# A hybrid decoder-layer step on one core: output projection in products of 512 columns, and three pieces of work moved behind the last token tile

## The chip, the core and the metric

The kernel runs on one NeuronCore of a Trainium2 chip. A core has five engines that run their own instruction queues in order: PE (TensorE, matrix products; its weight loads are listed as PEld), DVE (VectorE), ACT (ScalarE), POOL (GpSimd) and SP (SyncE, here only for starting transfers). ACT and POOL start transfers too. The metric is device microseconds (us) of one execution, as the median of the runs.

## The reference, cut to what matters

One inference step of one decoder layer, for a prompt of 512 tokens and a batch of 8 sequences with 8 new tokens each, so 576 token rows of width 1024. Two attention branches (`o_fox`, `o_nsa`) are computed first, from the inputs, the weights and a paged cache. What follows them is where the change lies:

```python
def post_mixer(x, pm, o_fox, o_nsa, lp):
    br_fox = jnp.einsum('btk,kd->btd', o_fox.reshape(b, t_len, FOX_QW), lp['w_br_fox'])
    br_nsa = jnp.einsum('btk,kd->btd', o_nsa.reshape(b, t_len, NSA_QW), lp['w_br_nsa'])
    mix = pm['g_fox'] * br_fox + pm['g_nsa'] * br_nsa
    x = x + pm['gt1'] * jnp.einsum('btd,de->bte', mix, lp['w_out'])
    h = rms_norm(x, lp['norm2_g']) * (1.0 + pm['sc2']) + pm['sh2']
    u = jax.nn.relu(jnp.einsum('btd,df->btf', h, lp['w_up']))
    return x + pm['gt2'] * jnp.einsum('btf,fd->btd', u * u, lp['w_down'])
```

`w_out` is 1024 x 1024, `w_up` 1024 x 4096, `w_down` 4096 x 1024. All data are float32. The outputs are the two `y` and the new cache rows.

## The kernel before, in words

**Precision.** A float32 operand is cut into a high and a low part of the type that PE multiplies (`split`, line 131 for the low part on DVE, line 112 for the high part on ACT). A product is then three products: high by high, low by high and high by low. For the 64 sample tokens a tile of 128 rows holds high and low rows together, so that two products do.

**Stages.** Input projection, compressed keys, prompt attention, sample attention, gates and branches (`mix_part`), then the four that matter here: the output projection (`out_part`), the first quarter-way of up (`up_first`), the rest of up (`mlp_up`) and down (`mlp_down`).

**Output projection.** Five token tiles, in the order 0, 4, 1, 2, 3 (tile 4 holds the sample tokens; tile 3 is the last). The stationary operand is `mix2` (tokens), the moving one `w_out`. The weight comes in four parts `wo0` to `wo3`, each 256 columns by all eight 128-row blocks, with a high and a low half (`wo1h`, `wo1l`). A token tile makes four groups of products of 256 columns, each into a PSUM bank of its own, and after each group DVE multiplies the bank by the gate (`wot`) and adds it to the residual `x`. When a tile's four groups are done, its rows are stored (`x2D`, POOL's queue) and normalised: ACT sums the squares (`nsq`; for the last tile `n`), DVE runs a chain of 13 small instructions (`ntx` to `nrs`) for the inverse root and scales the rows. PE turns the result (`nt`) some groups later, ACT applies scale and shift (`nv`), and the pair is split into `h3H`, `h3L` or `h`, the operands of up. ACT also stores `nv` to DRAM (`hvD`).

**First features of up.** `up_first` computes features 0 to 767 as six parts of 128 (`wu1`, `wu2`, `wu3` hold two parts each), for two halves of 288 tokens. Parts 0 to 3 run first for the first half of the tokens, which needs tiles 0, 1 and a part of 4; between the second and the third of these PE turns the last tile (`nt<-identF,n`), and ACT writes its parts into a buffer `R`. Then parts 0 to 3 run for the second half (`h`, which needs tiles 2 and 3), then parts 4 and 5 (`wu3`, the late feature weights) for both halves. Each group of 24 products fills one of four PSUM banks, and ACT empties it into `u`. The raw weights (`wur`) come over SP's queue into three buffers, so the fourth load waits until the first part has been split.

**Token differences and sums.** The rest of up runs features in pairs of 128 by a scheme of seven products in place of eight. It needs differences of token quarters (`R<-R` and their splits `T0` to `T3`; `moving_sums`, line 2077) and sums of weight quarters (`sums<-pu`; `pair_weights`, line 2102). For the differences the parts of tiles 0, 1, 2 and 4 are read back from `hvD` into `R` by two transfers on POOL's queue; those of tile 3 are written by ACT.

**What sets the order.** The kernel is written in one order, and a scheduler that runs when the kernel is built places the instructions of each engine by a modelled timeline. Three things bind it: on PE a chain (`link`) that keeps products in the written order in these stages; `issue_after`, which puts an instruction behind a named one; and buffers, whose next writer waits for the last reader. `self.normed` names the two splits that a tile's `norm_parts` made last.

Of the kernel before, what the change touches and what calls it, by code (L numbers as in the profile page):

```python
# [6 lines left out]
F32 = mybir.dt.float32  # L7
# [4 lines left out]
OP = mybir.AluOpType  # L12
AX = mybir.AxisListType

P = 128
# [4 lines left out]
NS = 64  # L20
# [25 lines left out]
class Step:  # L46
# [86 lines left out]
    def rsqrt(self, out, ss, inv):  # L133

        sh = list(out.shape)
        tag = "_".join(map(str, sh[1:]))
        x, h, t = [self.small.tile(sh, F32, tag=f"nt{a}{tag}", name=f"nt{a}{self.turn}") for a in "xht"]
        i = self.small.tile(sh, I32, tag=f"nti{tag}", name=f"nti{self.turn}")
        self.turn += 2
        self.ts(x, ss, inv, EPS, OP.mult, OP.add)  # L140
        self.ts(h, x, -0.5, None, OP.mult)
        self.ts(i, x.bitcast(I32), 1, None, OP.logical_shift_right)
        self.ts(i, i, -1.0, float(0x5F3759DF), OP.mult, OP.add)
        y = i.bitcast(F32)
        for n in range(3):
            self.tt(t, y, y, OP.mult)
            self.tt(t, t, h, OP.mult)
            self.stt(out, t, 1.5, y, OP.add, OP.mult)
            y = out

# [644 lines left out]
    def rows_mm(self, pb, i, n, terms, c0=0):  # L795

        if i < 4:
            h, l = slice(P * i, P * i + P), slice(NT + NS + P * i, NT + NS + P * i + P)
            todo = [(a[:, s], w) for a, (wh, wl) in terms for s, w in ((h, wh), (l, wh), (h, wl))]
        else:  # L800
            todo = [(a[:, SEQ:SEQ + P], w) for a, ws in terms for w in ws]
        for c, (a, w) in enumerate(todo):
            self.mm(pb[:, 0:n], a, w, c == 0, c == len(todo) - 1)
# [1163 lines left out]
    def out_weights(self, q, raw=None, pin=None):  # L1967

        return self.stream(raw, self.cols(self.I["w_out"], 256 * q, 256), [P, NK, 256], "wo", q, raws=2 if raw else 0,
                           room=self.place_of(q, f"wo{q}", NK), pin=pin)  # L1970

    def out_part(self, pw, mix2, x2, h3):
# [8 lines left out]
        for i in (0, 4, 1, 2, 3):  # L1981
            m = TILES[i][1]
            for q in range(4):
                if (i, q) in turn_at:
                    rest.pop(turn_at[i, q])()
                c0 = 256 * q
                pb = self.mmb(f"wo{q}_{i}")
                self.rows_mm(pb, i, 256, [(mix2[:, k], (ws[q][0][:, k, :], ws[q][1][:, k, :])) for k in range(NK)])
                if g is None:
                    g = gp = self.gate_prompt(pw, 16, 0.5, "1")  # L1990
                t = pw.tile([P, 256], F32, tag="wot", bufs=2, name=f"wot{q}_{i}")
                if i < 4:
                    self.tt(t, pb[:, 0:256], g[:, c0:c0 + 256], OP.mult)
                else:
                    self.fold(t[:m], pb[:, 0:256], pw.tile([NS, 256], F32, tag="fold", bufs=1, name=f"fold{q}"))
                    self.tt(t[:m], t[:m], g[:m, c0:c0 + 256], OP.mult)
                self.tt(x2[:m, i, c0:c0 + 256], x2[:m, i, c0:c0 + 256], t[:m], OP.add)
# [12 lines left out]
    def up_first(self, pu, h3):  # L2010
# [4 lines left out]
        def weights(q):  # L2015
            return self.stream(None, self.cols(self.I["w_up"], P * q, P), [P, NK, P], "wu", f"{q}", raws=0,
                               parts=1, room=[w[:, NK * (q % 2):NK * (q % 2) + NK] for w in t[q // 2]])
# [11 lines left out]
        for grp in range(2):  # L2029
            for q in range(4):  # L2030
                up(q, grp, ws[q])
                if grp == 0 and q == 1:
                    R = self.pb.tile([P, NK, NT], F32, tag="x", bufs=1, name="R")
                    for h in range(2):
                        self.dma("gpsimd", R[:, 4 * h:4 * h + 4, 0:self.COL[3]], self.hvD[:, 4 * h:4 * h + 4])
                    self.norm_parts(3, h3, self.n3, lambda h: R[:, 4 * h:4 * h + 4, self.COL[3]:NT], False)
            if grp == 0:
                self.chain = None
        self.moving_sums(pu, R)
        ws = [weights(q) for q in range(4, 6)]  # L2040
# [36 lines left out]
    def moving_sums(self, pu, R):  # L2077
# [3 lines left out]
        for n, (out, a, b) in enumerate(((b11, b12, b11), (b12, b22, b12), (b22, b22, b11), (b21, b21, b22))):  # L2081
            self.tt(out, a, b, OP.subtract)
# [31 lines left out]
    def mlp_up(self, pu, h3):  # L2114
# [10 lines left out]
        def ready(n):  # L2125
            with ExitStack() as c:
                for i in (self.splits[-1], self.last_high) if n == FIRST + 1 else ():
                    c.enter_context(self.tc.issue_after(i))
# [311 lines left out]
```

## Time and profile before

| | |
|---|---|
| median of 3 runs | 1203.73 us (1199.81 to 1206.84) |
| the profiled execution | 1203.84 us |
| its span, first to last instruction | 1202.0 us |
| PE busy | 1156.1 us, 96% of the span |
| DVE, ACT, POOL busy | 770.0, 559.0, 154.7 us |
| mean granted PE clock | 0.991 |

Times in the trace run from the first instruction. A row of a timeline has the start, the time from start to end in us, the engine, the line, the operation, what it writes and reads, and how many instructions are merged; in brackets stands the idle time before it and what ended it. A row of a table by stretches of time has the stretch, its length, the busy time of each engine with the instructions that started in it, the PE clock that was granted (1.00 is full), the mean busy share of the 16 DMA engines and their rate. The chain of waits follows the work that ended last back to its start, and has a start, a length and what filled it.

### The profile page before, as it was taken

What the parts mean: (1) busy time and instruction counts of PE and PEld (TensorE: products, weight loads), DVE (VectorE), ACT (ScalarE), POOL (GpSimd) and SP (SyncE); (2) the same over time, 40 slices, a digit from 0 to 9 for tenths busy, and PEclk for the clock granted to TensorE, in tenths of its full rate; (3) what the DMA queues carried; (4) which work ended last, traced back from release to release, by engine and by line L of the source; (5) the groups of instructions that cost most, each with busy time, mean ns of one, the idle gap of its engine ahead of it and who ended that gap; (6) DMA issues with size and microseconds to landing.
All of it is one profiled execution on the core that took longest, in us unless ns stands there. A gap on an engine that the chain in (4) does not pass through costs nothing.

```text
span 1202.0 us, 24863 instructions
## 1 busy us (share of the span) xinstructions
PE 1156.1 (96%) x9335; PEld 1003.1 (83%) x9335; DVE 770.0 (64%) x1990; ACT 559.0 (47%) x1187; POOL 154.7 (13%) x172
## 2 busy tenths in 40 slices
PE   3899999999999999999999999998999999999998
PEld 3887789999666656777899999998999997888886
DVE  3678785685888856666543445667667844655586
ACT  2455463444777864545523233364556655222230
POOL 1012100000321130000300000001464500000000
PEclk9999999999999999999999999999999999999999
DMA  9599456896785348999863333354444545445302
GB/s 212 159 258 248 158 151 200 259 306 218 224 269 167 114 166 264 316 307 319 211 162 80 80 97 126 103 163 167 144 147 147 172 147 188 146 169 185 110 28 79
DMA packets 168826, 215.37 MB, mean 179 GB/s; under 512 B 18297, under 2 KB 140610, under 8 KB 166530
## 3 DMA queue, kind: packets, MB, share of 16 engines
q1 hardware_dynamic: 147650, 174.21, 46.6%
q0 software_dynamic: 9216, 25.16, 6.7%
q10 hardware_dynamic: 11840, 14.42, 4.0%
q8 instruction: 73, 1.20, 0.4%
q14 instruction: 47, 0.39, 0.1%
HBM read 190.11 MB, written 44.53 MB: 195 GB/s over the span
## 4 chain that ended last, share of the span: by engine, by line
PE 83%; DMA 5%; DVE 5%; SPq 3%; ACT 3%; issue 2%; ACTq 0%; DVEq 0%; POOLq 0%
PE dn L77 16%; PE z L77 9%; PE mg L77 8%; PE hid L77 6%; PE br L77 4%; PE wo L77 4%; PE ss L77 2%; SPq L155 2%; PE up L77 2%; PE ct L83 2%; PE k L83 2%; DMA cpg<-in_cache_nsa_kv 2%; PE ada L77 2%; PE so L77 2%; PE sp L83 1%
## 5 line engine op out<-in xcount | busy, mean ns | idle before, releaser
L77 PE MATMUL z<-winh,h 128*128 128x264 f32 (+1 forms) x576 | 110.9, 286 | 0.3
L77 PEld LDWEIGHTS z<-winh,h 128*128 128x128 f32 x576 | 91.7, 190 | 2.1 <-DVE h L787 0.9
L77 PE MATMUL z<-winl,h 128*128 128x264 f32 (+1 forms) x320 | 88.1, 284 | 0.0
L112 ACT ACTIVATE xh<-ct 128x256 fp32r<-128x256 f32 x128 | 48.0, 385 | 61.1 <-PE ct L83 36.4
L77 PE MATMUL mg<-hH,wml 128*128 128x288 f32 x256 | 75.3, 296 | 0.9 <-DVE wml L131 0.9
L77 PE MATMUL mg<-hH,wmh 128*128 128x288 f32 x256 | 75.3, 296 | 0.0
L100 DVE TENSOR_TENSOR acc<-acc,dn 128x512 f32<-128x512 f32 x60 | 41.2, 687 | 49.4 <-PE dn L77 49.3
L77 PE MATMUL mg<-hL,wmh 128*128 128x288 f32 x256 | 72.6, 294 | 0.0
L131 DVE TENSOR_TENSOR xl<-ct,xh 128x256 fp32r<-128x256 f32 x128 | 51.6, 420 | 16.6 <-ACT xh L112 14.8
L77 PEld LDWEIGHTS z<-winl,h 128*128 128x128 f32 x320 | 60.6, 190 | 0.0
L83 PE MATMUL ct<-identF,ro 128*128 128x128 f32 x256 | 37.1, 286 | 22.4 <-DVE ro L115 22.2
L131 DVE TENSOR_TENSOR wml<-wmr,wmh 128x1024 fp32r<-128x1024 f32 x14 | 17.1, 1225 | 55.9 <-ACT wmh L112 55.9
L83 PEld LDWEIGHTS ct<-identF,ro 128*128 128x128 f32 x256 | 30.7, 149 | 25.3 <-DVE ro L115 18.7
L77 PEld LDWEIGHTS mg<-hH,wml 128*128 128x128 f32 x256 | 48.1, 188 | 1.1 <-DVE wml L131 1.1
L77 PEld LDWEIGHTS mg<-hH,wmh 128*128 128x128 f32 x256 | 48.1, 188 | 0.2
L77 PEld LDWEIGHTS mg<-hL,wmh 128*128 128x128 f32 x256 | 47.2, 188 | 0.1
L131 DVE TENSOR_TENSOR wp<-sums,wp 128x1024 fp32r<-128x1024 f32 x26 | 38.2, 1474 | 11.7 <-ACT wp L112 10.9
L77 PE MATMUL hid<-xh,w1hlk 128*128 128x512 f32 (+1 forms) x160 | 45.4, 372 | 0.1
L77 PE MATMUL hid<-xh,w1hlv 128*128 128x512 f32 (+1 forms) x160 | 45.0, 367 | 0.5 <-ACT xh L112 0.4
L112 ACT ACTIVATE mgt<-mg 128x288 f32<-128x288 f32 x32 | 12.9, 410 | 58.5 <-PE mg L77 58.5
L112 ACT ACTIVATE u<-u 128x1152 f32<-128x1152 f32 x29 | 33.7, 1161 | 10.0 <-DVE u L100 9.3
L131 DVE TENSOR_TENSOR wp<-pu,wp 128x512 fp32r<-128x512 f32 (+1 forms) x26 | 27.2, 1050 | 16.9 <-ACT wp L112 16.9
(1163 smaller groups left out, 3644.3 us busy)
## 6 DMA issues: line engine op xcount, KB each, us to landing
adw<-in_w_ada SPq DMA_DIRECT2D x16, 1024.0 KB
foxD<-in_cache_fox_kv SPq DMA_DIRECT2D x128, 128.0 KB
wdr<-in_w_down SPq DMA_DIRECT2D x32, 512.0 KB
cpg<-in_cache_nsa_kv SPq DMA_DIRECT2D x120, 128.0 KB
fr<-foxD SPq DMA_DIRECT2D x28, 512.0 KB
sr<-in_cache_nsa_kv SPq DMA_DIRECT2D x112, 128.0 KB
pu<-in_w_up SPq DMA_DIRECT2D x26, 512.0 KB
uD<-u ACTq DMA_DIRECT2D x16, 576.0 KB
```

Source lines behind the costliest of these rows:

```text
L77: ins = self.nc.tensor.matmul(out, a, b, start=start, stop=stop, skip_group_check=True)
L83: ins = self.nc.tensor.transpose(out, in_, self.identF[:n, :n])
L100: self.nc.vector.tensor_tensor(out, a, b, op=op)
L112: return self.nc.scalar.activation(out, in_, f, **kw)
L131: self.splits.append((eng or self.nc.vector).tensor_tensor(l, x, h.bitcast(F32), op=OP.subtract).ins)
L155: self.issued[eng] = getattr(self.nc, eng).dma_start(out, in_).ins
```

## The change

It has four parts.

1. `out_weights`, `rows_mm`, `out_part`: the four parts of `w_out` are now 512 columns by four row blocks. Part q holds row half q % 2 and column half q // 2. A token tile makes two groups of products of 512 columns; each runs through two weight parts into one PSUM bank and is taken up once, by DVE instructions of 512 columns.
2. `up_first`: the weights of feature parts 4 and 5 (`wu3`) are written ahead of the token differences, and their splits are pinned behind `self.normed`, the last splits of the last token tile.
3. `moving_sums` and `ready`: the four token differences, and the first sums and weight splits of the pair scheme, are pinned behind the same instructions.
4. The two transfers from `hvD` to `R` (columns 0 to 447) become four: columns 0 to 319 (tiles 0, 1, 4) for both halves, then 320 to 447 (tile 2) for both.

```diff
+    def pinned(self, pins):
+        with ExitStack() as c:
+            for i in pins or ():
+                c.enter_context(self.tc.issue_after(i))
+            yield
...
     def out_weights(self, q, raw=None, pin=None):
-        return self.stream(raw, self.cols(self.I["w_out"], 256 * q, 256), [P, NK, 256], "wo", q, raws=2 if raw else 0,
-                           room=self.place_of(q, f"wo{q}", NK), pin=pin)
+        w = self.I["w_out"][:, 512 * (q % 2):512 * (q % 2) + 512]
+        return self.stream(raw, self.cols(w, 512 * (q // 2), 512), [P, 4, 512], "wo", q, raws=2 if raw else 0,
+                           room=self.place_of(q, f"wo{q}", 4), pin=pin)
...
-                pb = self.mmb(f"wo{q}_{i}")
-                self.rows_mm(pb, i, 256, [(mix2[:, k], (ws[q][0][:, k, :], ws[q][1][:, k, :])) for k in range(NK)])
+                if q % 2 == 0:
+                    pb = self.mmb(f"wo{q}_{i}")
+                self.rows_mm(pb, i, 512, [(mix2[:, 4 * (q % 2) + k], (ws[q][0][:, k, :], ws[q][1][:, k, :])) for k in range(4)],
+                             part=(q % 2, 2))
...
+                if q % 2 == 0:
+                    continue
+                t = pw.tile([P, 512], F32, tag="wot", bufs=2, name=f"wot{q}_{i}")
                 if i < 4:
-                    self.tt(t, pb[:, 0:256], g[:, c0:c0 + 256], OP.mult)
+                    self.tt(t, pb, g[:, cs], OP.mult)
...
-                    for h in range(2):
-                        self.dma("gpsimd", R[:, 4 * h:4 * h + 4, 0:self.COL[3]], self.hvD[:, 4 * h:4 * h + 4])
+                    for a, e in ((0, self.COL[2]), (self.COL[2], self.COL[3])):
+                        for h in range(2):
+                            self.dma("gpsimd", R[:, 4 * h:4 * h + 4, a:e], self.hvD[:, 4 * h:4 * h + 4, a:e])
...
+        ws = [weights(q, self.normed) for q in range(4, 6)]
         self.moving_sums(pu, R)
-        ws = [weights(q) for q in range(4, 6)]
...
-            self.tt(out, a, b, OP.subtract)
+            with self.pinned(self.normed):
+                self.tt(out, a, b, OP.subtract)
...
-            with ExitStack() as c:
-                for i in (self.splits[-1], self.last_high) if n == FIRST + 1 else ():
-                    c.enter_context(self.tc.issue_after(i))
+            with self.pinned((self.splits[-1], self.last_high) if n == FIRST + 1 else self.normed if n == FIRST else ()):
```

How the instructions stand on three engines, of the kernel before and of the changed one.

PE in the first token tile of the output projection, before: the end of the first group (`wo0`), the turns for the gate (`gp`), the start of the second group.

```order
L77 MATMUL wo_0_10835<-wo0h,mix_9234 128x256 x2
L77 MATMUL wo_0_10835<-wo0l,mix_9234 128x256
L83 MATMUL gp_10861<-identF,modT 128x128 x4
L83 MATMUL gp_10867<-identF,modT 128x128 x4
L77 MATMUL wo_0_10876<-wo1h,mix_9234 128x256 x2
L77 MATMUL wo_0_10876<-wo1l,mix_9234 128x256
```

The same place in the changed kernel:

```order
L77 MATMUL wo_0_10835<-wo0h,mix_9234 128x512 x2
L77 MATMUL wo_0_10835<-wo0l,mix_9234 128x512
L83 MATMUL gp_10849<-identF,modT 128x128 x4
L83 MATMUL gp_10855<-identF,modT 128x128 x4
L77 MATMUL wo_0_10835<-wo1h,mix_9234 128x512 x2
L77 MATMUL wo_0_10835<-wo1l,mix_9234 128x512
```

The products are twice as wide and half as many, and those with `wo1` go on in the bank that those with `wo0` began (10835 in both).

ACT at the end of the output projection and the start of up, before: splits of the weights (`wu2h`, `wu3h`), the last tile's squares (`n`), tile 2's parts (`nv`, `h<-nv`, their stores), and the last tile's parts (`R<-nt`).

```order
L112 ACTIVATE wu2h<-wur_0_11665 128x1024
L112 ACTIVATE wu3h<-wur_0_11922 128x1024
L112 ACTIVATE n_10797,nss_3_11574<-x_10779 128x1024
L112 ACTIVATE nv_0_11600<-nt_20_11595,modT,coef_10833 128x128 x4
L112 ACTIVATE nv_1_11613<-nt_21_11608,modT,coef_10833 128x128 x4
L112 ACTIVATE wu3h<-wur_0_11926 128x1024
L112 ACTIVATE h_10790<-nv_0_11600 128x4x128
L155 DMA hvD<-nv_0_11600 128x4x128
L112 ACTIVATE h_10790<-nv_1_11613 128x4x128
L155 DMA hvD<-nv_1_11613 128x4x128
L112 ACTIVATE R<-nt_30_11724,modT,coef_10833 128x128 x4
L112 ACTIVATE R<-nt_31_11735,modT,coef_10833 128x128 x4
```

The same place in the changed kernel:

```order
L112 ACTIVATE wu2h<-wur_0_11395 128x1024
L112 ACTIVATE n_10797,nss_3_11304<-x_10779 128x1024
L112 ACTIVATE nv_0_11330<-nt_20_11325,modT,coef_10833 128x128 x4
L112 ACTIVATE nv_1_11343<-nt_21_11338,modT,coef_10833 128x128 x4
L112 ACTIVATE h_10790<-nv_0_11330 128x4x128
L162 DMA hvD<-nv_0_11330 128x4x128
L112 ACTIVATE h_10790<-nv_1_11343 128x4x128
L162 DMA hvD<-nv_1_11343 128x4x128
L112 ACTIVATE R<-nt_30_11456,modT,coef_10833 128x128 x4
L112 ACTIVATE R<-nt_31_11467,modT,coef_10833 128x128 x4
L112 ACTIVATE h_10790<-R 128x4x128 x2
L112 ACTIVATE wu3h<-wur_0_11634 128x1024
```

Both `wu3h` have moved from ahead of the last tile's parts to behind them; the second follows directly, and then five `u<-up`, which empty PSUM banks. Before, two of the `u<-up` stood between the two `h<-R`.

DVE from the last tile's scaling (`n`) on, before: the first weight sum, a `wu3` split, tile 2's splits (`h<-nv`), the first token difference (`R<-R`), the last tile's splits (`h<-R`), the next sum, and the split of the first difference (`T0l`).

```order
L104 TENSOR_SCALAR n_10797<-x_10779,nrs_3_11576 128x1024
L2102 TENSOR_TENSOR sums<-pu_0_12042 128x512
L131 TENSOR_TENSOR wu3l<-wur_0_11926,wu3h 128x1024
L131 TENSOR_TENSOR h_10790<-nv_0_11600,h_10790 128x4x128
L131 TENSOR_TENSOR h_10790<-nv_1_11613,h_10790 128x4x128
L100 TENSOR_TENSOR R<-R 128x4x288
L131 TENSOR_TENSOR h_10790<-R,h_10790 128x4x128 x2
L2102 TENSOR_TENSOR sums<-pu_0_12042,pu_1_12043 128x512
L131 TENSOR_TENSOR T0l<-R,T0h 128x1152
```

The same place in the changed kernel:

```order
L104 TENSOR_SCALAR n_10797<-x_10779,nrs_3_11306 128x1024
L131 TENSOR_TENSOR h_10790<-nv_0_11330,h_10790 128x4x128
L131 TENSOR_TENSOR h_10790<-nv_1_11343,h_10790 128x4x128
L131 TENSOR_TENSOR h_10790<-R,h_10790 128x4x128 x2
L2116 TENSOR_TENSOR sums<-pu_0_11774 128x512
L131 TENSOR_TENSOR wu3l<-wur_0_11634,wu3h 128x1024
L2116 TENSOR_TENSOR sums<-pu_0_11774,pu_1_11775 128x512
L131 TENSOR_TENSOR wu3l<-wur_0_11638,wu3h 128x1024
L100 TENSOR_TENSOR R<-R 128x4x288
```

All four splits of `h` now stand directly behind `n`, and the first token difference stands behind both `wu3` splits. The other `wu3l` stood ahead of the chain that leads to `n` before.

More of the change, by code (lines that the diff above doesn't have):

```diff
@@ L1 @@
-from contextlib import ExitStack, nullcontext
+from contextlib import ExitStack, contextmanager, nullcontext
 import concourse.bass as bass
@@ L149, in rsqrt @@
             y = out
+    @contextmanager
+    def pinned(self, pins):
[3 more added lines that the diff above has]
+            yield
     def dma(self, eng, out, in_):
@@ L793, in fold, with rows_mm @@
         self.tt(out, x[0:NS], t, OP.add)
-    def rows_mm(self, pb, i, n, terms, c0=0):
+    def rows_mm(self, pb, i, n, terms, part=(0, 1)):
         if i < 4:
@@ L802, in rows_mm @@
         for c, (a, w) in enumerate(todo):
-            self.mm(pb[:, 0:n], a, w, c == 0, c == len(todo) - 1)
+            self.mm(pb[:, 0:n], a, w, c == part[0] == 0, c == len(todo) - 1 and part[0] == part[1] - 1)
     def zc(self, c0, n):
@@ L1985, in out_part @@
                     rest.pop(turn_at[i, q])()
-                c0 = 256 * q
-                pb = self.mmb(f"wo{q}_{i}")
-                self.rows_mm(pb, i, 256, [(mix2[:, k], (ws[q][0][:, k, :], ws[q][1][:, k, :])) for k in range(NK)])
+                cs = slice(512 * (q // 2), 512 * (q // 2) + 512)
+                if q % 2 == 0:
+                    pb = self.mmb(f"wo{q}_{i}")
+                self.rows_mm(pb, i, 512, [(mix2[:, 4 * (q % 2) + k], (ws[q][0][:, k, :], ws[q][1][:, k, :])) for k in range(4)],
+                             part=(q % 2, 2))
                 if g is None:
                     g = gp = self.gate_prompt(pw, 16, 0.5, "1")
-                t = pw.tile([P, 256], F32, tag="wot", bufs=2, name=f"wot{q}_{i}")
+                if q % 2 == 0:
+                    continue
+                t = pw.tile([P, 512], F32, tag="wot", bufs=2, name=f"wot{q}_{i}")
                 if i < 4:
-                    self.tt(t, pb[:, 0:256], g[:, c0:c0 + 256], OP.mult)
+                    self.tt(t, pb, g[:, cs], OP.mult)
                 else:
-                    self.fold(t[:m], pb[:, 0:256], pw.tile([NS, 256], F32, tag="fold", bufs=1, name=f"fold{q}"))
-                    self.tt(t[:m], t[:m], g[:m, c0:c0 + 256], OP.mult)
-                self.tt(x2[:m, i, c0:c0 + 256], x2[:m, i, c0:c0 + 256], t[:m], OP.add)
+                    self.fold(t[:m], pb, pw.tile([P, 512], F32, tag="wot", bufs=2, name=f"fold{q}")[:NS])
+                    self.tt(t[:m], t[:m], g[:m, cs], OP.mult)
+                self.tt(x2[:m, i, cs], x2[:m, i, cs], t[:m], OP.add)
             g = gp if i else self.gate_sample(pw, 16, 0.5, "1")
@@ L2013, in up_first, with weights @@
         us = [pu.tile([P, 2, NT], F32, tag="u", bufs=2, name=f"u{n}") for n in range(2)]
-        def weights(q):
+        def weights(q, pin=None):
             return self.stream(None, self.cols(self.I["w_up"], P * q, P), [P, NK, P], "wu", f"{q}", raws=0,
-                               parts=1, room=[w[:, NK * (q % 2):NK * (q % 2) + NK] for w in t[q // 2]])
+                               parts=1, room=[w[:, NK * (q % 2):NK * (q % 2) + NK] for w in t[q // 2]], pin=pin)
         def up(q, grp, w):
```

## The prediction

> **What bounds the kernel now.** I first read busy time by stretches, to see which engine sets the pace behind the change:
>
> ```profile
> 850.00:986.00 136.00, 136.00 (x1024) 136.00 (x1023) 91.77 (x114) 78.95 (x101) 61.16 (x40) 1.00 0.45 150
> ```
>
> The columns are PE, PE's weight loads, DVE, ACT and POOL, each with its instructions. In up's pair scheme PE is busy for all of the 136.00 us (1024 products, 0.133 us each) and DVE for 91.77. From there on PE is the clock of the kernel: what lets PE begin the pair scheme earlier moves the end by as much. So next I read the chain of waits from the end of the output projection on, where PE is not alone on it:
>
> ```profile
> 783.65 8.65 PE wo L77 x72
> ...
> 808.51 7.94 DMA R<-hvD
> ...
> 816.54 1.36 DVE R L100
> 817.90 0.62 DVE h L131
> ...
> 818.56 26.54 PE up L77 x186
> ...
> 1002.83 141.78 PE dn L77 x624
> ```
>
> For 7.94 us the path is a transfer into `R`; then come the token difference that reads it and the split `h` that stands behind it on DVE. PE's timeline shows what this stretch costs:
>
> ```profile
> 806.77 1.07 PE L83 MATMUL nt<-identF,n 128*128 128x128 f32 x8 [1.46 <-DVE n L104]
> ...
> 814.07 0.29 PE L77 MATMUL up<-h,wu1h 128*128 128x288 f32 x1
> ...
> 818.56 0.55 PE L77 MATMUL up<-h,wu1h 128*128 128x288 f32 x2 [3.53 <-DVE h L131]
> ```
>
> There are two idle times: 1.46 us before the last token tile is turned, and 3.53 us before the second half of the tokens (six products slipped in at 814.07). A third cost stands in the `up` products by stretches (PE, weight loads, ACT, then the granted clock):
>
> ```profile
> 818.56:822.27 3.71, 3.71 (x17) 3.71 (x18) 0.39 (x1) 0.55 0.09 27
> 822.27:826.03 3.76, 3.76 (x29) 3.76 (x29) 0.41 (x1) 0.99 0.00 0
> ```
>
> Behind the longer idle time PE had a granted clock of 0.55 for 3.71 us: 17 products, where the next 3.76 us hold 29. That lost 3.71 x 0.45 = 1.67 us.
>
> **Part 1: products of 512 columns.** 448 products become 224 (4 x 48 for the prompt tiles, 32 for the sample tile). Of 256 columns, 72 took 8.65 us, 0.120 each; of 512, in down, 624 took 141.78 us, 0.227 each. So 448 x 0.120 = 53.8 us becomes 224 x 0.227 = 50.9, which is 2.9 less. The two rows put about 13 ns beside each product's columns, whatever their number, and it is these that are halved. [...]
>
> Not all of the 2.9 us is had, because the first token tile meets weights that are still being split:
>
> ```profile
> 738.82:752.20 13.38, 13.16 (x106) 12.62 (x105) 11.39 (x17) 7.45 (x9) 0.00 (x0) 1.00 0.46 141
> 752.20:797.88 45.68, 45.68 (x386) 45.48 (x385) 30.73 (x107) 18.72 (x41) 2.26 (x4) 1.00 0.32 97
> ```
>
> Before, PE lost 0.22 us there and DVE was busy for 11.39 of 13.38.
>
> ```profile
> 742.17 2.36 DVE L131 TENSOR_TENSOR wo1l<-wor,wo1h 128x1024 fp32r<-128x1024 f32 x2
> L100 DVE TENSOR_TENSOR acc<-acc,dn 128x512 f32<-128x512 f32 x60 | 41.2, 687 | 49.4 <-PE dn L77 49.3
> ```
>
> From 742.17 on DVE makes six splits of 1.18 us and, among them, one pair of 512 columns at 687 ns an instruction, in the new order: `wo1l` twice, `wo2l`, `wot`, `wo2l`, `x`, `wo3l` twice. PE starts at 738.82, has `wo0` and the turns `gp` behind it at 742.4, and then waits about 0.5 us for the first `wo1l` (there at 743.4), 0.4 for the second `wo2l` (747.9) and 0.4 for the first `wo3l` (749.7). It leaves the tile at 752.0 in place of 752.20, with next to no gain. The other tiles have 176 products for 352: 42.3 - 40.0 = 2.3 us, so the last tile ends at 795.3 in place of 797.88, 2.6 us earlier. Bounds: 1.5 if the waits double, 3.2 if there are none. DVE's pairs of 512 columns are no load on the way: ten pairs at 2 x 0.69 us take the place of twenty of half the width; ACT's folds of the sample tile, two for four, lie beside PE's products too.
>
> **Up to the turn of the last tile.** SP, DVE and ACT before:
>
> ```profile
> 794.55 0.37 SPq L181 DMA_DIRECT2D wur<-in_w_up  x1
> 796.35 1.83 SPq L181 DMA_DIRECT2D wur<-in_w_up  x2
> ```
>
> ```profile
> 793.29 1.23 DVE L131 TENSOR_TENSOR wu1l<-wur,wu1h 128x1024 fp32r<-128x1024 f32 x1
> ...
> 803.50 0.15 DVE L106 TENSOR_SCALAR ntx<-nss 128x1 f32<-128x1 f32 x1
> ```
>
> ```profile
> 798.75 1.06 ACT L112 ACTIVATE wu2h<-wur 128x1024 fp32r<-128x1024 f32 x1 [2.61 <-DMA wur<-in_w_up]
> 801.27 1.06 ACT L112 ACTIVATE wu3h<-wur 128x1024 fp32r<-128x1024 f32 x1 [1.45 <-DMA wur<-in_w_up]
> 802.23 1.05 ACT L112 ACTIVATE n<-x 128x1024 f32<-128x1024 f32 x1
> ```
>
> ACT stood at `wu3h` until its load had come, with `n` queued behind it, and DVE's chain to the scaled tile (`ntx` at 803.50) behind both. Now `n` follows the second `wu2h`, which takes the fourth `wur` load. SP starts that load when the first `wu1l` is done, 794.55 before. PE is through with `wo1` of the last tile some 2 us earlier, so `wu1l` runs from 791.4 and the load starts at 792.6; it took 4.2 us (794.55 to 798.75), so `wu2h` starts at 796.8 and `n` at 797.85, 4.4 us earlier. DVE goes to `ntx` when the second `wu2l` is done, at 799.1. From `ntx` to PE's turn it took 3.27 us (803.50 to 806.77), so the tile is ready at 802.4. PE is there at 795.3 + 0.8 for a turn + 48 x 0.133 = 802.5. The 1.46 us are gone by a hair; bounds 0 and 1.46.
>
> **The second half of the tokens.** ACT behind `n`, before:
>
> ```profile
> 803.27 1.84 ACT L112 ACTIVATE nv<-nt,modT,coef 128x128 f32<-128x128 f32 x5
> ...
> 806.02 1.09 ACT L112 ACTIVATE wu3h<-wur 128x1024 fp32r<-128x1024 f32 x1
> ...
> 808.01 2.94 ACT L112 ACTIVATE R<-nt,modT,coef 128x128 f32<-128x128 f32 x8
> 810.75 0.71 ACT L112 ACTIVATE h<-R 128x512 fp32r<-128x512 f32 x1
> ```
>
> From `nv` to `R<-nt` are 4.74 us, about 1.0 of it the second `wu3h`, which now comes later. So `nv` starts at 798.9, `R<-nt` at 802.7, and both `h<-R` of ACT are done by 807. DVE's `h<-R` waits for these alone, no longer behind `R<-R` and its transfer, and ends by 808. PE wants it at 802.5 + 7.3 (806.77 to 814.07) = 809.8. The 3.53 us go, and with them the 1.67 of the clock; 1.8 us are to spare. Bounds: 3.2 and 5.2 together.
>
> What is late next, on each queue that the moved work now stands in? The last splits of the first pair's sums stand here on DVE, before:
>
> ```profile
> 833.33 2.47 DVE L131 TENSOR_TENSOR wp<-sums,wp 128x1024 fp32r<-128x1024 f32 x2 [1.48 <-ACT wp L112]
> ```
>
> - ACT: both `wu3h` (1.06 us each) stand ahead of `u<-up`, and the first `u<-up` frees the bank for PE's fifth group. Free at 808.8, wanted at 809.8.
> - DVE: behind `h<-R` come two sums and two `wu3l`, 3.8 us, to 812; PE wants `wu3` at 822.5. Then come differences, `T` and first sums. Before, 19.3 us passed from the first `R<-R` (816.54) to the end of the row above (835.8). From 812 that is 831 at the latest; PE reaches the pair scheme's first such product at about 837 (818.56 + 26.54 + 1.6 - 9.3). Slack 6 us.
> - POOL: four `R` issues for two, with nothing behind them but sums for the third pair. The last two wait for the `hvD` stores that ACT issues at about 803, and land near 811; their reader comes at 812 and has the slack above.
> - SP: the order of its transfers is the same, the loads of `w_out` in rows twice as long.
>
> **The sum.** 2.6 + 1.46 + 3.53 + 1.67 = 9.3 us, against a profiled execution of 1203.84 us (its span 1202.0, 1.8 around it), which is 0.1 above the median of the runs. 1203.8 - 9.3 = 1194.5.
>
> **Rivals.**
>
> *The late weights hold the banks.* This one can end on the other side. The last two `wur` loads now share the DMA engines with the first two `R` transfers, 1.31 MB, which POOL can issue from 797.6 on. If the sixth load lands after 808.3, ACT stands at `wu3h` with `u<-up` behind it, and PE waits for a bank: a us for a us, and 1.67 more for the clock once the idle time is like the 3.53. Against it: before, the sixth load was issued at 797.8 (the two SP rows above) and ACT took it at 806.02 without a wait, so 8.2 us at most; now it is issued at about 795.7. For it:
>
> ```profile
> 797.00:818.56 21.56, 16.58 (x128) 16.14 (x126) 11.97 (x27) 13.30 (x29) 2.06 (x3) 1.00 0.90 289
> ```
>
> The DMA engines were busy for 0.90 of this stretch, at 289 GB/s, of which 1.31 MB are 4.5 us. At worst 795.7 + 8.2 + 4.5 = 808.4, just the point. [...] A wait of 2 to 4 us gives 1196.5 to 1200; no gain is left from a landing at 816 on (7.6 us of wait and the clock), and 0.5% slower takes 822. Chance 0.12, a quarter of it slower.
>
> *The fourth load stays the bound.* If it takes 5.7 us in place of 4.2, the 1.46 us stay: 1196.0. For it, the margin is 0.1 us; against it, as before only its followers are in flight with it. Chance 0.12.
>
> *Nothing fixed in a product.* [...] Chance 0.03.
>
> *The pair scheme gives it back.* If DVE is 11 us later than I have it, not 6, PE waits 5 us at its first pairs: 1199.5, and 1201 with the clock. Chance 0.05.
>
> **How the numbers follow.** The forecast has the other 0.68. Half a per cent, 6 us, is about what a measurement of this kernel can tell from no change (its runs lie between 1199.81 and 1206.84). From the bounds of the terms, the gain is 1.5 + 0 + 3.2 = 4.7 to 3.2 + 1.46 + 5.2 = 9.9 us, so 1199.0 to 1193.8; with 2.5 us for the spread of runs below and 1 above, 1191 to 1200, which takes in the second and third rival and most of the first. Faster by over 0.5% means below 1197.7: 0.9 of the forecast's chance, 0.7 of the fourth load's, 0.3 of the banks', half of the third's, 0.75 in all. Slower 0.03, the same 0.22.
>
> **What would show it.** Right: `wo` as 224 products near 0.227 us, its last tile ending near 795.3; no idle time of PE over 0.5 us before the turn of `n` or before `up<-h`; a granted clock of 1.00 from 800 to 840; `up3a` starting near 835.7 in place of 845. Wrong: idle time of PE that ends in `u<-up` or `wu3l`; idle time in the pair scheme, which has none now; waits in the first token tile far above 1.3 us together, or products of 512 columns far from 0.227 us.

## The result, and the profile after

The changed kernel takes 1194.58 us (median of 4 runs, 1193.61 to 1195.16) against 1203.74 (4 runs, 1199.81 to 1206.84). The ratio is 0.9924, with a 95% interval of 0.9907 to 0.9941. The forecast was 1194.5. The profiled execution took 1193.61 us, with a span of 1191.8.

The chain of waits behind the output projection has no transfer and no DVE left in it:

```profile
781.10 13.63 PE wo L77 x60
795.61 6.39 PE up L77 x48
802.87 31.97 PE up L77 x240
...
841.23 1.60 PE up3b L77 x12
...
992.58 141.81 PE dn L77 x624
```

240 products of up follow each other without a break, where before 186 of them stood behind `R<-hvD`. PE's timeline at the three places of the forecast (no brackets: no idle time in front):

```profile
794.57 1.03 PE L83 MATMUL nt<-identF,nsq 128*128 128x128 f32 x8
...
801.83 1.03 PE L83 MATMUL nt<-identF,n 128*128 128x128 f32 x8
...
809.11 0.29 PE L77 MATMUL up<-h,wu1h 128*128 128x288 f32 x1
```

By stretches (columns as in the prediction): the output projection behind its first token tile, the first features of up, and the pair scheme, where PE is busy for all of 136.00 us, as before. (The first row starts 0.15 us late. From the start of the turns `gs`, 750.93, where the prediction's row starts too, it is 43.64 us against 45.68.)

```profile
751.08:794.57 43.49, 43.49 (x209) 35.79 (x207) 29.02 (x89) 18.44 (x39) 2.26 (x4) 1.00 0.33 98
...
802.87:834.84 31.97, 31.97 (x242) 31.97 (x242) 25.95 (x26) 21.18 (x36) 7.87 (x5) 1.00 0.57 186
839.60:975.60 136.00, 136.00 (x1024) 136.00 (x1023) 94.27 (x117) 78.92 (x101) 61.42 (x40) 1.00 0.45 152
```

ACT now has `n` directly behind the second `wu2h`, and both `wu3h` behind both `h<-R`:

```profile
796.17 1.06 ACT L112 ACTIVATE wu2h<-wur 128x1024 fp32r<-128x1024 f32 x1 [3.29 <-DMA wur<-in_w_up]
797.13 1.05 ACT L112 ACTIVATE n<-x 128x1024 f32<-128x1024 f32 x1
...
805.22 1.19 ACT L112 ACTIVATE h<-R 128x512 fp32r<-128x512 f32 x2
806.26 2.04 ACT L112 ACTIVATE wu3h<-wur 128x1024 fp32r<-128x1024 f32 x2
808.16 1.55 ACT L112 ACTIVATE u<-up 128x288 f32<-128x288 f32 x4
```

On DVE `h<-R` no longer stands behind `R<-R`. The rows of 837.29 and 840.14 will be needed later:

```profile
795.59 0.69 DVE L100 TENSOR_TENSOR x<-x,wot 128x512 f32<-128x512 f32 x1
797.26 1.23 DVE L131 TENSOR_TENSOR wu2l<-wur,wu2h 128x1024 fp32r<-128x1024 f32 x1 [0.98 <-ACT wu2h L112]
...
805.92 1.30 DVE L131 TENSOR_TENSOR h<-R,h 128x512 fp32r<-128x512 f32 x2 [3.02 <-ACT h L112]
...
813.44 1.36 DVE L100 TENSOR_TENSOR R<-R 128x1152 f32<-128x1152 f32 x1 [1.52 <-DMA R<-hvD]
...
815.79 1.36 DVE L100 TENSOR_TENSOR R<-R 128x1152 f32<-128x1152 f32 x1 [0.39 <-DMA R<-hvD]
...
837.29 2.92 DVE L131 TENSOR_TENSOR wp<-pu,wp 128x512 fp32r<-128x512 f32 x2
840.14 0.45 DVE L100 TENSOR_TENSOR u<-up3b,sums 128x288 f32<-128x288 f32 x1
```

The last row empties a PSUM bank. PE begins to fill it again with:

```profile
841.07 0.43 PE L77 MATMUL up3b<-T2h,wp 128*128 128x288 f32 x2
```

The two profiled executions differ by 10.23 us, and 1.14 of that are not the change's: the branch products ahead of the output projection already start at 734.67 in place of 735.81. It is a loss of PE's clock in the stage of the compressed keys, which the execution of before had and the one of after had not. Up to there the execution of before was 0.56 us ahead: PE comes out of the same idle time at 317.00 before and at 317.56 after. The stretch (PE, granted clock, DMA share, rate), before:

```profile
317.00:320.50 3.50, 3.50 (x26) 0.53 0.98 295
```

and after, where the first 0.56 us of it are still idle:

```profile
317.00:320.50 3.50, 2.94 (x30) 1.00 0.80 261
```

3.50 us at 0.53 cost 1.65, about the 0.56 and the 1.14 together. So single executions are compared by a distance inside the trace: from the start of the last 24 branch products (the last row `PE br L77 x24` of the chain) to the start of the first products of `up5a`, from where on nothing waits on the changed work in any run. The two rows of before:

```profile
735.81 3.19 PE br L77 x24
...
864.28 1.60 PE up5a L77 x12
```

and of after:

```profile
734.67 3.19 PE br L77 x24
...
854.01 1.60 PE up5a L77 x12
```

128.47 us against 119.34.

### The profile page after: what moved, and what is told of

Read it like the earlier page. It is cut to its first block, busy times and chain, and to the rows that moved or that the text cites. A ratio compares the mean times of both kernels' runs of the same rounds, so it can differ in the third digit from the quotient of the medians.

```text
span 1191.8 us, 24394 instructions
## 1 busy us (share of the span) xinstructions
PE 1149.2 (96%) x9111; PEld 986.7 (83%) x9111; DVE 767.8 (64%) x1968; ACT 558.7 (47%) x1185; POOL 159.6 (13%) x174
## 3 DMA queue, kind: packets, MB, share of 16 engines
q8 instruction: 72, 1.18, 0.4%
## 4 chain that ended last, share of the span: by engine, by line
PE 81%; DVE 6%; DMA 5%; ACT 3%; SPq 3%; issue 2%; ACTq 0%; DVEq 0%
PE dn L77 17%; PE mg L77 9%; PE z L77 6%; PE hid L77 5%; PE br L77 4%; PE wo L77 4%; PE up L77 3%; SPq L162 3%; PE ss L77 3%; PE so L77 2%; PE k L83 2%; PE ct L83 2%; DMA cpg<-in_cache_nsa_kv 2%; PE ada L77 1%; PE sp L83 1%
## 5 line engine op out<-in xcount | busy, mean ns | idle before, releaser
L77 PE MATMUL z<-winh,h 128*128 128x264 f32 (+1 forms) x576 | 111.0, 286 | 0.3
L77 PEld LDWEIGHTS z<-winh,h 128*128 128x128 f32 x576 | 91.7, 190 | 2.1 <-DVE h L794 0.9
L77 PE MATMUL z<-winl,h 128*128 128x264 f32 (+1 forms) x320 | 88.2, 284 | 0.5 <-DVE winl L131 0.5
L77 PE MATMUL mg<-hH,wml 128*128 128x288 f32 x256 | 75.4, 296 | 0.9 <-DVE wml L131 0.9
L77 PE MATMUL mg<-hH,wmh 128*128 128x288 f32 x256 | 75.4, 296 | 0.0
L77 PE MATMUL mg<-hL,wmh 128*128 128x288 f32 x256 | 72.6, 294 | 0.0
L77 PEld LDWEIGHTS z<-winl,h 128*128 128x128 f32 x320 | 60.6, 190 | 0.7 <-DVE winl L131 0.7
L77 PEld LDWEIGHTS mg<-hH,wml 128*128 128x128 f32 x256 | 48.1, 188 | 1.1 <-DVE wml L131 1.1
L77 PEld LDWEIGHTS mg<-hH,wmh 128*128 128x128 f32 x256 | 48.1, 188 | 0.2
L77 PEld LDWEIGHTS mg<-hL,wmh 128*128 128x128 f32 x256 | 47.2, 188 | 0.1
L77 PE MATMUL hid<-xh,w1hlv 128*128 128x512 f32 (+1 forms) x160 | 44.7, 365 | 0.7 <-ACT xh L112 0.5
L77 PE MATMUL hid<-xh,w1hlk 128*128 128x512 f32 (+1 forms) x160 | 44.6, 367 | 0.1
L131 DVE TENSOR_TENSOR wp<-pu,wp 128x512 fp32r<-128x512 f32 (+1 forms) x26 | 30.2, 1167 | 14.7 <-ACT wp L112 14.7
L77 PE MATMUL br<-oH,wbh 128*128 128x288 f32 x128 | 37.8, 296 | 0.2 <-ACT mgt L112 0.2
```

The source lines that it names most:

```text
L77: ins = self.nc.tensor.matmul(out, a, b, start=start, stop=stop, skip_group_check=True)
L131: self.splits.append((eng or self.nc.vector).tensor_tensor(l, x, h.bitcast(F32), op=OP.subtract).ins)
```

## Experiments

The theory: the four terms of the sum (wo 2.6, idle time before the turn of the last tile 1.46, idle time before the second half of the tokens 3.53, the clock behind it 1.67) are separate, each undone by its own edit. The rival: the edits lean on each other, since the order is set by a scheduler and PE's own place moves too. The distances:

| run | from | to `up5a` | distance | against before | ratio of the times, 95% interval |
|---|---|---|---|---|---|
| before | 735.81 | 864.28 | 128.47 | | |
| after | 734.67 | 854.01 | 119.34 | -9.13 | 0.9924 (0.9907 to 0.9941) |
| wide_only | 735.62 | 859.02 | 123.40 | -5.07 | 0.9942 (0.9913 to 0.9971) |
| order_only | 736.12 | 859.16 | 123.04 | -5.43 | 0.9964 (0.9947 to 0.9982) |
| no_pin_weights | 738.59 | 861.68 | 123.09 | -5.38 | 0.9922 (0.9900 to 0.9943) |
| no_pin_sums | 737.95 | 857.78 | 119.83 | -8.64 | 0.9917 (0.9885 to 0.9949) |
| halves | 738.98 | 861.60 | 122.62 | -5.85 | 0.9959 (0.9940 to 0.9979) |
| quarters | 735.52 | 902.15 | 166.63 | +38.16 | one execution |
| weights_pin_only | 733.15 | 852.51 | 119.36 | -9.11 | 0.9924 (0.9897 to 0.9951) |
| r_unsplit | 736.05 | 855.38 | 119.33 | -9.14 | 0.9932 (0.9904 to 0.9959) |
| first_tiles_mixed | 735.01 | 857.38 | 122.37 | -6.10 | 0.9937 (0.9912 to 0.9961) |
| halves_weights_pin | 738.70 | 860.25 | 121.55 | -6.92 | one execution |
| weights_pin_256 | 734.21 | 860.71 | 126.50 | -1.97 | 0.9991 (0.9967 to 1.0014) |
| diff_pin_256 | 735.47 | 858.63 | 123.16 | -5.31 | 0.9964 (0.9944 to 0.9984) |

Each distance is that of one profiled execution, with what the clock lost inside it. Three programs that take the same time there (after, weights_pin_only, r_unsplit) give 119.33 to 119.36, so the distance repeats within 0.03 us. The whole times are much coarser, since they carry the clock losses elsewhere: no_pin_weights is 3.75 us longer than the changed kernel by the distance, and not told from it by the ratio (0.9922 and 0.9924).

**wide_only: the products of 512 columns alone.** `rows_mm`, `out_weights` and `out_part` are the changed ones, the rest is as before:

```diff
-        ws = [weights(q, self.normed) for q in range(4, 6)]
         self.moving_sums(pu, R)
+        ws = [weights(q) for q in range(4, 6)]
...
-            with self.pinned(self.normed):
-                self.tt(out, a, b, OP.subtract)
+            self.tt(out, a, b, OP.subtract)
...
-                    for a, e in ((0, self.COL[2]), (self.COL[2], self.COL[3])):
+                    for a, e in ((0, self.COL[3]),):
```

and `ready` without its new pin.

> Only the products of 512 columns are changed; the weights, the token differences, the first sums and R's transfers stand as before. Theory (the four terms are separate): the last token tile of the output projection ends 2.2 to 2.6 us earlier, but the late weights' split still stands ahead of n on ACT and R's wait ahead of the second h on DVE, so both idle times of PE (near 1.5 and 3.5 us) and the low granted clock behind the second stay, and the gain is 2 to 3 us in all. Rival (the idle times are lost to products that are too narrow, and the order only follows): both idle times go with the products, and the gain is 7 us or more.

Measured: 5.07 us, more than the theory allows and less than the rival. PE's timeline and the chain:

```profile
804.65 1.06 PE L83 MATMUL nt<-identF,n 128*128 128x128 f32 x8 [1.68 <-DVE n L104]
...
816.44 0.53 PE L77 MATMUL up<-h,wu1h 128*128 128x288 f32 x2 [1.94 <-DVE h L131]
```

```profile
816.44 23.41 PE up L77 x174
```

Both idle times are there. But of the 192 products of this stretch only 174 stand behind the second wait, where before it was 186: the scheduler now lets PE do 18 products of the second half ahead of the wait, not 6. These 12 are 1.6 us, by which the idle time is shorter, and behind 1.94 us of it the granted clock stayed at 1.00 (174 products in 23.41 us, 0.135 each; the 240 of the changed kernel took 0.133 each). So the terms are not separate. That the clock stayed up here is in part luck (the last section).

**order_only: parts 2 to 4, with products of 256 columns.** The three functions of part 1 are those of before:

```diff
-                self.rows_mm(pb, i, 512, [(mix2[:, 4 * (q % 2) + k], (ws[q][0][:, k, :], ws[q][1][:, k, :])) for k in range(4)],
-                             part=(q % 2, 2))
+                self.rows_mm(pb, i, 256, [(mix2[:, k], (ws[q][0][:, k, :], ws[q][1][:, k, :])) for k in range(NK)])
```

> Only the order and R's four transfers are changed; the products keep 256 columns. Theory: both idle times and the low clock go, 1.46 + 3.53 + 1.67 = 6.7 us, and wo keeps its time, so the gain is 6 to 7 us. Rival (the gains need each other): with wo 2.2 us later PE is also later, so an idle time that is gone here by the order alone leaves nothing to gain from wo, and the two runs' gains do not sum to 9.1; by that rival this run gains 8 or more or 4 or less.

Measured: 5.43 of 6.7, between the theory and the rival. The second idle time is gone, but 0.64 us of the first are left, and a new wait stands in the pair scheme:

```profile
806.28 1.06 PE L83 MATMUL nt<-identF,n 128*128 128x128 f32 x8 [0.64 <-ACT h L112]
...
846.11 0.54 PE L77 MATMUL up3b<-T2h,wp 128*128 128x288 f32 x2 [0.42 <-DVE u L100]
```

DVE shows why the first stays. With pairs of 256 columns the last sum of `x` stands behind the second `wu2l`:

```profile
800.22 1.23 DVE L131 TENSOR_TENSOR wu2l<-wur,wu2h 128x1024 fp32r<-128x1024 f32 x1 [1.40 <-ACT wu2h L112]
801.37 0.42 DVE L100 TENSOR_TENSOR x<-x,wot 128x256 f32<-128x256 f32 x1
```

and ACT's `n` waits for it:

```profile
801.82 1.06 ACT L112 ACTIVATE n<-x 128x1024 f32<-128x1024 f32 x1 [1.63 <-DVE x L100]
```

In the changed kernel that sum was done ahead of `wu2l` (the rows of 795.59 and 797.26 above). The theory named the right wait, but it is part 1 and the hold on the weights together that remove it.

**no_pin_weights: the changed kernel without the hold on the late weights.**

```diff
-        ws = [weights(q, self.normed) for q in range(4, 6)]
         self.moving_sums(pu, R)
+        ws = [weights(q) for q in range(4, 6)]
```

> The changed kernel, but the last two splits of up's first weights are not held behind the last token tile's parts. Theory: ACT's wu3h stands ahead of n again and waits there for its load, so PE waits before the turn of the last tile, longer than the 1.46 us of before since PE is there 2 us earlier (2.5 to 4 us), and the second half of the tokens stays without an idle time over 1 us; 2.5 to 4 us slower than the changed kernel. Rival (fourth load is the bound, not the order): n is no later than now, and the time stays within 1 us.

Measured: 3.75 us more than the changed kernel, the theory's number, but not by its way alone. The wait before the turn is back and longer than before, since PE is there earlier, but it is 1.97 us, not 2.5 to 4; the rest is the clock, which falls behind it in this execution:

```profile
807.89 1.94 PE L83 MATMUL nt<-identF,n 128*128 128x128 f32 x8 [1.97 <-DVE n L104]
```

```profile
809.50:811.00 1.50, 1.50 (x8) 1.50 (x7) 1.18 (x2) 1.50 (x6) 0.00 (x0) 0.50 1.06 327
```

**no_pin_sums: the changed kernel without the hold on the first pair's sums.**

```diff
-            with self.pinned((self.splits[-1], self.last_high) if n == FIRST + 1 else self.normed if n == FIRST else ()):
+            with self.pinned((self.splits[-1], self.last_high) if n == FIRST + 1 else ()):
```

> The changed kernel, but the first pair's sums of up's weights are not held back: one of them stands between the parts of h on DVE. Theory: it waits for its load, which landed at 808.1 in the changed kernel, with both h<-R behind it, so the second half of the tokens begins 1 to 4 us late with an idle time of PE ending in DVE's h; if that idle time is over 3 us the granted clock falls behind it for 1 to 2 us more. 1 to 5 us slower. Rival (PE's second half is bound by ACT's u and h, not by DVE's order): no idle time, and the time is the changed kernel's within 0.5 us.

Measured: 0.49 us more, the rival's number and not the theory's 1 to 5. DVE does wait for the load, with both `h<-R` behind it, and it costs PE next to nothing:

```profile
811.08 0.69 DVE L2116 TENSOR_TENSOR sums<-pu 128x512 f32<-128x512 f32 x1 [5.53 <-DMA pu<-in_w_up]
```

```profile
813.04 0.54 PE L77 MATMUL up<-h,wu1h 128*128 128x288 f32 x2 [0.23 <-DVE h L131]
```

DVE's wait of 5.53 us left 0.23 us of idle time on PE.

**halves: each product of 512 columns issued as two of 256.** Layout, DVE's pairs and order stay those of the changed kernel.

```diff
-            self.mm(pb[:, 0:n], a, w, c == part[0] == 0, c == len(todo) - 1 and part[0] == part[1] - 1)
+            for o in (range(0, n, n // 2) if part[1] == 2 else [0]):
+                e = o + (n // 2 if part[1] == 2 else n)
+                self.mm(pb[:, o:e], a, w[:, o:e], c == part[0] == o == 0, c == len(todo) - 1 and part[0] == part[1] - 1)
```

> The changed kernel in everything (weights' layout, DVE's pairs of 512 columns, order), but each product of 512 columns is issued as two of 256 into the halves of the same bank: 448 products again. Theory (what is saved in wo is a fixed price beside each product's columns): the last tile ends 2.2 us later than in the changed kernel, measured from the branch products ahead of wo, as late as before; there is still no idle time before the turn of the last tile, because DVE's last sum of x stands ahead of the second wu2l, where the run with the order alone had 256 columns there and 0.64 us of idle time; pair scheme 2.2 us later than in the changed kernel. Rival (wo is faster by its layout or by fewer evictions, not by the number of products): wo stays within 0.5 us of the changed kernel's.

Measured: the last tile ends 62.08 us behind the branch products (801.06), where it is 59.90 in the changed kernel and 62.07 before: 2.18 us, the whole gain of part 1 in the output projection. Each product here has its own weight load, as in before (9335 products, 9335 loads); whether the price is the product's or the load's the run does not tell. There is no idle time before the turn, as expected of DVE's order. Not expected was 1.1 us in the pair scheme:

```profile
808.33 1.04 PE L83 MATMUL nt<-identF,n 128*128 128x128 f32 x8
...
848.54 0.53 PE L77 MATMUL up3b<-T2h,wp 128*128 128x288 f32 x2 [0.82 <-DVE u L100]
```

```profile
845.20 2.92 DVE L131 TENSOR_TENSOR wp<-pu,wp 128x512 fp32r<-128x512 f32 x2
848.04 0.44 DVE L100 TENSOR_TENSOR u<-up3b,sums 128x288 f32<-128x288 f32 x1
```

PE waits for a bank that DVE reads only behind the second pair's splits.

**quarters: four products of 128 columns.** As halves, with `n // 4` in place of `n // 2`.

> As halves, but four products of 128 columns each: 896 products. Theory (13 ns beside the columns, whatever their number): 128 columns at 0.053 + 0.013 = 0.066 us each, so wo's products take 59.5 us in all, 6 us more than with 256. Rival (something that comes with each product, such as the loading of its weights, has a floor above that): a product of 128 columns takes 0.1 us or more, and wo becomes 35 us longer or more.

Measured: the rival. PE's timeline merges four products a row:

```profile
762.48 0.61 PE L77 MATMUL wo<-wo0h,mix 128*128 128x128 f32 x4
762.92 0.61 PE L77 MATMUL wo<-wo0l,mix 128*128 128x128 f32 x4
```

762.48 to 762.92 is 0.44 us for four: 0.11 each, hardly less than with 256 columns. The 13 ns beside the columns fit 256 (0.120), 288 (0.133) and 512 columns (0.227); carried on to 128, the rows of 256 and 512 would give 0.066. The run does not show what sets the 0.11.

**weights_pin_only: products of 512 columns and the hold on the late weights, without the three other edits.** The changed kernel with the edit of no_pin_sums, and:

```diff
-            with self.pinned(self.normed):
-                self.tt(out, a, b, OP.subtract)
+            self.tt(out, a, b, OP.subtract)
...
-                    for a, e in ((0, self.COL[2]), (self.COL[2], self.COL[3])):
+                    for a, e in ((0, self.COL[3]),):
```

> The changed kernel without three of its edits: the token differences and the first sums are not held back, and R comes in two transfers as before; the products of 512 columns and the hold on the late weights stay. Theory: three of the first pair's sums stand on DVE ahead of both h<-R, and wait for loads that landed at 808 and later in the changed kernel, so the second half of the tokens begins 2 to 5 us late with idle time of PE that ends in DVE's h, and the granted clock falls behind it where the idle time is over 2 us: 2 to 6 us slower than the changed kernel. Rival (the hold on the weights does it all, the rest has slack): no idle time, the time within 1 us of the changed kernel's.

Measured: 0.02 us from the changed kernel. The rival is right, and more than that: the other three edits gain nothing here. DVE's timeline:

```profile
805.72 0.69 DVE L2115 TENSOR_TENSOR sums<-pu,pu 128x512 f32<-128x512 f32 x1 [2.07 <-DMA pu<-in_w_up]
...
807.06 1.28 DVE L131 TENSOR_TENSOR h<-R,h 128x512 fp32r<-128x512 f32 x2
...
810.00 1.35 DVE L100 TENSOR_TENSOR R<-R 128x1152 f32<-128x1152 f32 x1
...
836.62 0.46 DVE L100 TENSOR_TENSOR u<-up3b,sums 128x288 f32<-128x288 f32 x1 [0.24 <-PE up3b L77]
```

The sums stand ahead of `h<-R` and wait, and `h` is still in time. `R<-R` stands behind `h<-R` without being held there. And `u<-up3b` waits for PE, not PE for it.

**r_unsplit: the changed kernel with R in two transfers.**

```diff
-                    for a, e in ((0, self.COL[2]), (self.COL[2], self.COL[3])):
+                    for a, e in ((0, self.COL[3]),):
```

> The changed kernel with R in two transfers in place of four. Theory (R's later reader has slack, and the holds keep it behind h on DVE): no idle time of PE at the second half of the tokens; the differences start 1 to 3 us later and the first pair's sums too, within their slack; the time within 1 us of the changed kernel's. Rival (the split is what lets R land before the pair scheme): the first pair's weights come after PE wants them, with idle time of PE at up3a or up3b and 1 to 4 us slower.

Measured: the theory's time, within 0.01 us, but not its account. The first difference does not start 1 to 3 us later but 2.06 earlier (78.77 us behind the branch products in the changed kernel, 76.71 here). POOL's queue shows why. In the changed kernel:

```profile
797.27 1.52 POOL L162 DMA_DIRECT2D R<-hvD  x2 [0.16 <-ACT wu2h L112]
809.04 0.75 POOL L162 DMA_DIRECT2D R<-hvD  x1 [10.25 <-DMA hvD<-nv]
```

and here:

```profile
806.16 1.52 POOL L162 DMA_DIRECT2D R<-hvD  x2 [7.69 <-DMA hvD<-nv]
```

ACT issued the first of the `hvD` stores that POOL waits for at 799.70 there and at 800.99 here. With R in four transfers, two of them go out just ahead of the stores, and the stores are waited for 9.3 us; with R in two it is 5.2. DVE is done with the first `u<-up3b` 104.50 us behind the branch products here and 105.92 there. So part 4 costs DVE 1.4 us of slack and gains nothing.

**halves_weights_pin: halves without the three other edits.** The diffs of halves and of weights_pin_only together.

> The run halves without three edits: token differences and first sums are not held back, R comes in two transfers. Theory (these edits make DVE 2.4 us later at the second pair's sums and take nearly all slack there, which is why halves lost 1.1 us in the pair scheme): the last tile ends as in halves, there is no idle time of PE before the turn, none in the pair scheme, and the fifth up pair's products begin 1.1 us earlier than in halves. Rival (the pair scheme's wait comes with the later end of wo, whatever the order): the wait at up3b stays, 0.8 us or more.

Measured: the theory. The wait at `up3b` is gone, and the fifth pair begins 1.07 us earlier than in halves. So the holds on differences and sums and the split of R together are what brings DVE late to the second pair.

**weights_pin_256 and diff_pin_256: before with one hold alone.** The first:

```diff
-        self.moving_sums(pu, R)
-        ws = [weights(q) for q in range(4, 6)]
+        ws = [weights(q, self.normed) for q in range(4, 6)]
+        self.moving_sums(pu, R)
```

The second:

```diff
-            self.tt(out, a, b, OP.subtract)
+            with self.pinned(self.normed):
+                self.tt(out, a, b, OP.subtract)
```

> The kernel before with the hold on the late weights alone; products of 256 columns. Theory: half of the first idle time goes (0.64 us of 1.46 stay, as in the run with the order alone, since DVE's last sum of x still stands behind the second wu2l), and R<-R stays ahead of h on DVE, so the second idle time stays near 3.5 us with its low clock: 0.8 to 1.5 us gained. Rival (this hold frees the second half of the tokens too, as it did beside the products of 512): no second idle time over 1 us, 5 us or more gained.

> The kernel before with the hold on the token differences alone; products of 256 columns. Theory: both h<-R stand ahead of R<-R, so the second idle time and its low clock go, 3.53 + 1.67 = 5.2 us, while wu3h stays ahead of n on ACT and the first idle time stays at 1.46: about 5 us gained. Rival (what waits next takes its place): the pair scheme's first sums or differences are late, or h is late for another reason, and 3 us or less are gained.

Measured: 1.97 and 5.31 us. The first is more than its theory has and far from its rival; the second is its theory's. With the hold on the weights alone both idle times shrink, to 0.49 and 2.71, and the clock falls behind the second:

```profile
804.21 1.06 PE L83 MATMUL nt<-identF,n 128*128 128x128 f32 x8 [0.49 <-ACT h L112]
...
814.90 0.85 PE L77 MATMUL up<-h,wu1h 128*128 128x288 f32 x2 [2.71 <-DVE h L131]
```

The scheduler leaves `R<-R` ahead of `h<-R` here, where beside products of 512 columns the same hold puts it behind. The hold on the differences alone removes the second idle time and the clock's loss, 3.53 + 1.67, and leaves the first at 1.46, as its theory says.

**first_tiles_mixed: weights_pin_only, with the first token tile and the sample tile in turns.** The turn of the first tile stands one weight part later.

```diff
-        rest, turn_at = {}, {(1, 1): 0, (2, 0): 4, (2, 3): 1}
-        for i in (0, 4, 1, 2, 3):
+        rest, turn_at = {}, {(1, 2): 0, (2, 0): 4, (2, 3): 1}
+        for i, b in [(0, 0), (4, 0), (0, 1), (4, 1)] + [(i, b) for i in (1, 2, 3) for b in range(2)]:
```

> The kernel with the products of 512 columns and the hold on the late weights alone, and beside that the first token tile and the sample tile of the output projection take turns by halves of the columns, so that PE wants the third and fourth part of w_out 3.6 us later; the turn of the first tile stands one part later. Theory (what wo lost of its forecast gain is PE waiting for the splits of these weights in the first tile): no labelled idle time of PE behind the first wo1, the last tile ends 0.3 to 0.5 us earlier, from the branch products ahead of wo, and so does everything behind it; by the time alone that is hardly to be told. Rival (these weights are no later than their products, and wo's remainder is something else): the last tile ends within 0.1 us of where it does in the changed kernel, or later because a turn now waits for its norm.

Measured: 3.01 us worse than weights_pin_only. The waits behind the first `wo1` went: the turn of the first tile starts 29.10 us behind the branch products, where it is 27.15 in the changed kernel, with 12 products more in front of it, which are 2.73 us; so 0.78 were saved. But the sample tile's norm is now late for its turn:

```profile
764.11 1.03 PE L83 MATMUL nt<-identF,nsq 128*128 128x128 f32 x8
...
772.88 0.68 PE L83 MATMUL nt<-identF,nsq 64*128 64x64 f32 x8 [2.26 <-DVE nsq L104]
```

and the clock fell behind that. So PE did wait for these splits, as the theory says, but the last tile does not end earlier and the version is worse. With that turn some parts later it might be 0.7 us better; that was not run. No run beats the changed kernel; weights_pin_only equals it with one hold in place of three.

## Why the prediction was right, and where it was not

The forecast of the whole was 9.3 us; measured by the distance it is 9.13, and in the medians 9.16. From start to start on PE the 9.13 fall into 2.17 up to the end of the last tile, 1.63 up to its turn, 3.71 up to the second half of the tokens and 1.61 up to `up3a`, for 2.6, 1.46, 3.53 and 1.67. The mechanism of each term came, but that the sum is within 0.2 us is in part luck: the output projection gave 0.4 less, and the two idle times 0.17 and 0.18 more each than the brackets say. (A bracket counts from the end of the last product, 0.29 us after its start, where the next one starts after 0.13.) The terms:

- *Output projection*, 2.6: it was 2.17 (62.07 to 59.90), within its bounds. The first tile gained 0.13 for 0.2, the rest 2.04 for 2.3. That it is the number of products was right: halves loses it all. A product took 0.120 us at 256 columns, 0.227 at 512 and 0.11 at 128. The sum of the chances has half of the third rival (*nothing fixed in a product*) as faster; no run shows the time behind that. What the runs showed is that the layout of 512 columns with 448 products (halves) ends 2.18 us later.
- *The turn of the last tile*, 1.46: gone. The margin was as narrow as forecast: DVE was done with `n` at 801.53, PE came at 801.83. What the forecast did not see is that with products of 256 columns the hold on the weights leaves 0.49 (weights_pin_256) or 0.64 (order_only); the rest comes from the wider pair of DVE, done ahead of `wu2l`.
- *The second half of the tokens and the clock*, 3.53 + 1.67: gone, both. The hold on the differences removes them by itself (diff_pin_256), as argued. But beside part 1 and the hold on the weights it is not needed, and the sum of the single gains (5.07 for part 1 and 5.43 for the rest) is 10.5, not 9.13. The size was right; the bookkeeping by edit was not.
- *"Slack 6 us"* in the pair scheme: mis-sized. The forecast followed DVE to the first pair's splits, which were in time (828.1; in the forecast 831 at the latest). The tight place is one pair on: `u<-up3b` stands behind the second pair's splits and was done at 840.59 (the row of 840.14), and PE began to fill that bank again at 841.07. That is 0.48 us of slack, so that nothing was lost here is close to luck. In order_only and in halves, where the output projection is 2.2 us longer, it was gone, and the way of the rival "the pair scheme gives it back", at 0.05, was taken there in small, with idle times of 0.42 and 0.82 us. One cause is a transfer: the forecast had the second transfers into `R` land near 811. ACT issued the stores of `hvD` at 799.70 and 801.09, earlier than forecast, but POOL, which waits for them, could issue the transfers only at 809.04 and 810.79, and their readers started at 813.44 and 815.79. r_unsplit shows that this lateness comes with part 4.
- *Late weights hold the banks*, *the fourth load*: did not come. Both `wu3h` ran at 806.26 without a wait, and the fourth load took 4.2 us (issued at 791.97, used at 796.17), as forecast.

Settled by runs: that the fixed price of a product, 13 ns between 256 and 512 columns, is the gain in the output projection, that the hold on the weights and part 1 together give all of the gain, that the other three edits give none beside them and cost DVE its slack, 1.4 us of it by the split of R. Open: why the output projection behind its first tile is 0.26 us short of the products' own 2.30, and what sets the 0.11 us of a product of 128 columns.

## What to carry to other kernels

Where a scheduler sets the order, an edit's worth depends on the other edits: measure each alone and each left out, by a distance inside the trace that repeats to hundredths of a us, not by whole times that scatter by 7 us (1199.81 to 1206.84 before). When an idle time goes, follow the engine that was moved past the first reader it feeds, to every bank it still has to read; the slack that counts is the smallest on that way. And an idle time of PE should be priced with the clock behind it as a chance, not as a sum: here the clock fell behind 2.15 us in one execution and stayed up behind 2.15 us in another.

## What the runs showed of the hardware

The granted clock fell behind idle times of PE shorter than 3.53 us, and not always. Where PE was busy without a break up to the idle time, the clock stayed at 1.00 behind 1.46 us (before, diff_pin_256) and behind 1.68 and 1.94 (wide_only; the eight turns behind 1.68 took 1.06 us, where they took 1.94 behind 1.97 in no_pin_weights), and fell to 0.50 behind 1.97 (no_pin_weights), 2.26 (first_tiles_mixed), 2.71 (weights_pin_256) and 3.53 (before). At the start of down it fell to 0.50 behind 2.15 us in diff_pin_256, and stayed at 1.00 behind 2.15 in weights_pin_256 and 1.90 in halves_weights_pin. So near 2 us both came in these runs. The fall behind 3.53 us lasted 3.42 us (818.94 to 822.36, at 0.50), which is 1.7 us lost.

In the stage of the compressed keys an idle time of 1.24 us was enough in before (0.50 from 317.18 to 320.60) and in halves_weights_pin (0.61 for the first 1.50 us, 0.50 for the next 2.00). In after, weights_pin_256 and diff_pin_256 the clock stayed at 1.00 behind the same 1.24 us. There PE had been half idle already: in the 3.00 us up to the end of that idle time it was busy for 1.18 in before and after, so 1.82 were idle in all.
